# A two-layer fp32 decoder trunk on one core: statistics after the first lead product, and four plain chunks in the first feed-forward layer

## The chip, the core and the metric

The kernel runs on one core of a Trainium2 chip. The core has five engines, each with an instruction queue that it works off in order: TensorE (PE, matrix products into the PSUM banks), VectorE (DVE), ScalarE (ACT), GpSimd (POOL) and SyncE (SP, which here only starts transfers). They wait for one another through semaphores, and DMA queues bring data from memory to SBUF. The metric is the device time of one execution in microseconds (us); the time of a kernel is the median over its runs.

## The reference

All of it is float32, for 512 positions of 1024 channels:

```python
def reference(x, attn_norm, w_qkv, w_attn_out, pool_norm, w_pool_in, w_pool_group, pool_scale,
              ffn_norm, w_ffn_gate_up, w_ffn_down, final_norm):
    for i in range(DEPTH):                       # DEPTH = 2
        j = i // N_MIXERS                        # N_MIXERS = 2
        if i % N_MIXERS == 0:
            x = x + dilated_attention_mixer(rmsnorm(x, attn_norm[j]), w_qkv[j], w_attn_out[j])
        else:
            x = x + pooling_mixer(rmsnorm(x, pool_norm[j]), w_pool_in[j], w_pool_group[j], pool_scale[j])
        x = x + swiglu_ffn(rmsnorm(x, ffn_norm[i]), w_ffn_gate_up[i], w_ffn_down[i])
    return rmsnorm(x, final_norm)

def rmsnorm(x, g):
    y = x * lax.rsqrt(jnp.mean(x * x, axis=-1, keepdims=True) + RMS_EPS)
    return y * g

def swiglu_ffn(h, w_gate_up, w_down):            # 1024 -> 2 x 2816 -> 1024
    gu = h @ w_gate_up
    return (jax.nn.silu(gu[..., :D_FF]) * gu[..., D_FF:]) @ w_down
```

The attention mixer projects to queries, keys and values of three groups of 8 heads, attends in bands of three dilations and merges the groups. The pooling mixer projects 1024 to 1024, takes trailing means over 2, 4, 8 and 16 positions less the token for four groups of 256 channels, and maps each group by a 256 x 256 matrix.

## The kernel before

**Layout.** The activations stand transposed: eight blocks X[k] of 128 channels (partitions) by 512 positions. A normed input is never formed as such ahead of a product. The products take x times the norm's gain, and since the reciprocal root mean square is one number per position, that is per column, the results are multiplied by a row vector, named row, when they are taken out of PSUM. So a product can start before its statistics are known; only its result has to wait for row.

**Precision.** Every operand of PE is split into a high part (named hi, or whi for weights) and the rest (lo, wlo), both in a reduced format, and each product is three matmuls: whi x hi, whi x lo, wlo x hi (L272, L273, L275 in a plain product, L391 to L393 in a Strassen one). ACT makes the high part (L96), DVE the low one (L97).

**Two ways to multiply.** A plain product (Product, L253) of 8 blocks is 24 matmuls of 512 columns. A chunk of the feed-forward's up side, 128 hidden channels, needs a gate and an up product, so 48 matmuls. In the Strassen form (chain, L453) the same chunk is seven multiplications of 12 matmuls with 256 columns. Its weights come as sums of blocks of the matrix (Pair, L140): three loads by SP and one by POOL that adds into a buffer already loaded (L158), and DVE additions (L173, L174). Its inputs are sums and differences of the fully normed blocks: prepare(k), k = 0 to 3, makes them for blocks k and k + 4. It writes normed blocks hp and their sums tp (L501 to L508), and splits them into the operands tb, tt (two) and tn. They need row, and DVE and ACT work on them while PE does plain chunks. NPLAIN says how many of the 22 chunks are plain, before the Strassen ones. The multiplications of a chain run in the PSUM banks sum, ps and seed, and are taken out by ACT and DVE (half, gt, up).

**Weights** go through rings of buffers: 5 split blocks w, 2 halves, 4 raw blocks, 2 raw halves. pump() lets the next load and the next split start when a buffer is free, and is called after each product and each multiplication.

**Statistics.** While a block of x is completed, note (L322) makes its hi and lo operands (named h, in L318 and L319; for layer 3 n) and adds its square into acc (L310). rstd (L329) then sums acc over the partitions with four matmuls against ones (L335). DVE adds the epsilon (var, L340) and POOL raises to the power -0.5 (rcol, L342), which gives 512 numbers as [128 x 4]. spread (L345) brings them with four matmuls into a [128 x 512] tile in PSUM, and ACT copies that to row (L356).

**The entries.** A layer begins with begin (L359), which starts products over those blocks that are ready, and finish (L362): it completes them, takes the statistics, starts a third product with three blocks, does the spread, and completes the third. There are three such entries: to the feed-forward of layer 0 (L1151), to the pooling mixer (L1179) and to the feed-forward of layer 1 (L1239). In the text the pooling entry is the second.

```python
    def finish(lead, layer, ks):
        for f in lead:
            f.add(ks)
        r = rstd([acc[layer]])
        lead += begin(1, layer, range(3))
        row = row_of(spread(r))
        lead[-1].add(range(3, KC))
        return row
```

**What sets the order.** The code issues instructions in program order, and a scheduler of the framework (tile) places those of each engine, by its own model of when operands are ready, into the five queues; tc.issue_after pins the instructions issued in it behind a named one. On the chip each queue then runs strictly in that order. So a part that is issued elsewhere also moves its neighbours on the other engines.

Of the kernel before, what the change touches and what calls it, by code (L numbers as in the profile page):

```python
# [18 lines left out]
KC = D // P  # L19
# [17 lines left out]
K2 = KC // 2  # L37
NPLAIN = 5
WARM = 6
# [12 lines left out]
def trunk(ctx: ExitStack, tc: tile.TileContext, xT, norms, w_first, w_qk, w_qkp, w_v0, w_v0p, w_v12, w_out, w_pair, w_down, w_down0, w_down1, w_down2, w_pin, w_pgrp,  # L52
          consts, ident_in, invcnt_in, outT):
    nc = tc.nc
# [171 lines left out]
    def ffn_plan(layer):  # L226
        blocks = (w_down0, w_down1, w_down2)
        for g, (first, stop) in enumerate(GROUPS):
            for j in range(first + (g > 0), stop + 1 if g < 2 else FC):
                if j < NPLAIN:  # L230
                    plain_gu(layer, j)
                else:
                    pairs(w_pair[layer, j])
            if g < 2:
                for i in range(K2):
                    pairs(blocks[g][layer, i])
        for kind, i in TURNS:
            if kind == "block":
                pairs(blocks[2][layer, i])
            else:  # L240
                plain(w_down[layer, i])
# [11 lines left out]
    class Product:  # L253
# [7 lines left out]
        def add(self, ks, cols=slice(0, S), pos=None):  # L261
            for k in ks:
                if self.w:
                    w, c = self.w, k if pos is None else pos + k
                else:
                    self.held, c = self.held or weights(), k
                    w = self.held.t
# [6 lines left out]
                self.done += 1  # L274
                nc.tensor.matmul(self.p[:, cols], w[1][:, s], mh[:, cols], start=False, stop=self.done == self.n)  # L275
            if not self.w:
# [85 lines left out]
# [6 lines that stand above are left out]
        row = row_of(spread(r))  # L368
        lead[-1].add(range(3, KC))
        return row  # L370

    def both(t):
# [557 lines left out]
    with tc.tile_pool(name="fpool", bufs=1) as fpool:  # L930
# [16 lines left out]
        def ffn(layer, nxt, lead, row, wk):  # L947
# [85 lines left out]
            def plain_pair(j):  # L1033
# [3 lines left out]
                pu = gu()  # L1037
                if j == NPLAIN - 1:
                    for k in range(KC):
                        give((op, k))  # L1040
# [83 lines left out]
            for g, (first, stop) in enumerate(GROUPS):  # L1124
                for j in range(first + (g > 0), stop + 1 if g < 2 else FC):
                    if j < NPLAIN:
                        plain_pair(j)
                        if j < K2:
                            prepare(j)
                    else:  # L1130
                        strassen_pair(j)
# [18 lines left out]

        lead = begin(2, 1, range(KC - 1))  # L1151
        row = finish(lead, 1, [KC - 1])
        with tc.tile_pool(name="work0", bufs=1) as wk:
# [19 lines left out]
        with tc.tile_pool(name="pooling", bufs=6) as wk:  # L1173
# [4 lines left out]

            lead = begin(2, 2, range(KC - 1))  # L1179
            row = finish(lead, 2, [KC - 1])  # L1180
            Y = {}

# [197 lines left out]
```

## Time and profile before

| | |
|---|---|
| three timed runs | 1251.72, 1253.34, 1253.52 us; median 1253.34 |
| profiled execution | 1251.78 us; span 1250.0 us, mean granted PE clock 0.996 |
| PE | 1237.6 us busy, 99%, 9072 matmuls |
| DVE | 1013.6 us busy, 81% |
| ACT | 679.7 us busy, 54% |
| POOL | 154.9 us busy, 12% |
| transfers | 189.91 MB, mean 152 GB/s |

How to read the rows below. An instruction's row holds its start in us from the start of the span, its duration in us (of the first, with its time until the last ends, where several are put together with x), the engine, the line of the kernel, the operation, out<-in by the program's names, shapes, and in brackets how long the engine had been idle before and what released it. In the list of waits on PE the three numbers are the idle time in us in all, the number of waits, and the longest. In the table of stretches each engine has its busy time in us and the number of its instructions; the last two numbers are the DMA engines' mean share and the GB/s. SPq and POOLq are the engines' transfer queues. Since matmuls overlap one another, their own durations are longer than the distance at which they follow each other; a rate is taken from starts.

### The profile page before, as it was taken

Reading aid. Unit: us, or ns where it says so; the run is one execution under the profiler, and the core shown is the slowest. Engines: PE = TensorE matmul, PEld = TensorE weight load, DVE = VectorE, ACT = ScalarE, POOL = GpSimd, SP = SyncE. Lnnn points to the kernel's source line nnn. Section 1 sums busy time; section 2 is a strip of 40 time slices with the busy share of each in tenths; the row PEclk is TensorE's granted clock in tenths of the full one; section 3 lists DMA queues with packets and bytes.
Section 4 is the critical chain, followed back from the end, with each engine's and each line's share of the span. In section 5 each row is a group of like instructions: output and inputs, shape, how many; then the busy total and the mean of one; then the engine's idle time right before and its main releaser. Section 6 shows DMA issues by size and latency. Waiting matters only on the chain. (4 is left out here: it accounts for less than half of the span.)

```text
span 1250.0 us, 23243 instructions
## 1 busy us (share of the span) xinstructions
PE 1237.6 (99%) x9072; PEld 1174.0 (94%) x9072; DVE 1013.6 (81%) x1687; ACT 679.7 (54%) x1171; POOL 154.9 (12%) x147
## 2 busy tenths in 40 slices
PE   9999999999999999999999999999999999999997
PEld 7889999999999988889999999988789999999997
DVE  7987788878778846798777878798989877888876
ACT  6444554445455544466466557563446646656652
POOL 2011111112111010101111111000310111111100
PEclk9999999999999999999999999999999999999998
DMA  8336566655756434437776786653144777677742
GB/s 291 110 85 170 134 156 145 163 131 159 182 132 161 132 138 136 113 81 194 187 186 158 177 208 163 153 181 118 51 119 117 182 182 178 153 205 190 174 116 68
DMA packets 76719, 189.91 MB, mean 152 GB/s; under 512 B 7600, under 2 KB 15936, under 8 KB 76608
## 3 DMA queue, kind: packets, MB, share of 16 engines
q1 hardware_dynamic: 51696, 142.26, 35.7%
q0 software_dynamic: 24336, 45.63, 22.5%
q8 instruction: 71, 1.16, 0.4%
q10 hardware_dynamic: 576, 0.52, 0.1%
q14 instruction: 40, 0.33, 0.1%
HBM read 186.29 MB, written 2.10 MB: 151 GB/s over the span
## 5 line engine op out<-in xcount | busy, mean ns | idle before, releaser
L96 ACT ACTIVATE whi<-raw 128x1024 fp32r<-128x1024 f32 (+2 forms) x315 | 318.7, 1016 | 248.3 <-PE seed L392 76.1
L97 DVE TENSOR_TENSOR wlo<-raw,whi 128x1024 fp32r<-128x1024 f32 (+2 forms) x315 | 367.1, 1169 | 105.3 <-ACT whi L96 104.5
L158 POOL DMA_DIRECT2D raw<-w_pair x34 | 41.1, 1209 | 310.5 <-ACT whi L96 75.4
L391 PE MATMUL sum<-tt,whi 128*128 128x256 f32 x272 | 77.0, 283 | 1.5 <-ACT seed L477 0.8
L392 PE MATMUL sum<-tt,whi 128*128 128x256 f32 x272 | 76.7, 282 | 0.0
L393 PE MATMUL sum<-tt,wlo 128*128 128x256 f32 x272 | 76.5, 281 | 0.0
L96 ACT ACTIVATE halfhi<-rawhalf 128x512 fp32r<-128x512 f32 (+1 forms) x87 | 53.2, 612 | 19.8 <-PE sum L392 12.4
L173 DVE TENSOR_TENSOR raw<-raw 128x512 f32<-128x512 f32 (+1 forms) x87 | 57.6, 662 | 2.1 <-issue 2.0
L174 DVE TENSOR_TENSOR raw<-raw 128x512 f32<-128x512 f32 (+1 forms) x87 | 57.7, 663 | 0.2
L97 DVE TENSOR_TENSOR halflo<-rawhalf,halfhi 128x512 fp32r<-128x512 f32 (+1 forms) x87 | 57.6, 664 | 0.0
L158 POOL DMA_DIRECT2D raw<-w_down x24 | 28.9, 1206 | 215.2 <-DMA raw<-w_down 34.4
L391 PEld LDWEIGHTS sum<-tt,whi 128*128 128x128 f32 x272 | 51.4, 189 | 1.9 <-ACT seed L477 1.0
L477 ACT COPY seed<-sum 128x256 f32<-128x256 f32 x58 | 20.8, 359 | 57.7 <-PE sum L393 57.5
L392 PEld LDWEIGHTS sum<-tt,whi 128*128 128x128 f32 x272 | 51.3, 189 | 0.0
L393 PEld LDWEIGHTS sum<-tt,wlo 128*128 128x128 f32 x272 | 51.2, 188 | 0.0
L391 PE MATMUL sum<-hz,whi 128*128 128x256 f32 x160 | 45.4, 284 | 0.5 <-ACT seed L477 0.3
L392 PE MATMUL sum<-hz,whi 128*128 128x256 f32 x160 | 45.3, 283 | 0.0
L392 PE MATMUL seed<-hy,whi 128*128 128x256 f32 x160 | 45.3, 283 | 0.0
L393 PE MATMUL seed<-hy,wlo 128*128 128x256 f32 x160 | 45.2, 283 | 0.0
L393 PE MATMUL sum<-hz,wlo 128*128 128x256 f32 x160 | 45.2, 283 | 0.0
L391 PE MATMUL seed<-hy,whi 128*128 128x256 f32 x160 | 45.1, 282 | 0.0
L158 POOL DMA_DIRECT2D raw<-w_qkp x18 | 22.0, 1222 | 166.4 <-DMA raw<-w_qkp 102.1
(610 smaller groups left out, 4631.7 us busy)
## 6 DMA issues: line engine op xcount, KB each, us to landing
raw<-w_pair SPq DMA_DIRECT2D x78, 512.0 KB, 4.7
raw<-w_qkp SPq DMA_DIRECT2D x36, 512.0 KB, 4.6
raw<-w_pair POOLq DMA_DIRECT2D x34, 512.0 KB, 7.6
raw<-w_down SPq DMA_DIRECT2D x32, 384.0 KB, 3.9
raw<-w_v SPq DMA_DIRECT2D x18, 512.0 KB, 4.1
raw<-w_qkp POOLq DMA_DIRECT2D x18, 512.0 KB, 7.4
rawhalf<-w_pair SPq DMA_DIRECT2D x34, 256.0 KB, 4.5
raw<-w_down SPq DMA_DIRECT2D x16, 512.0 KB, 4.9
```

The lines of the kernel that those rows point to most:

```text
L96: nc.scalar.activation(hi, v, AF.Copy)
L97: nc.vector.tensor_tensor(lo, v, hi.bitcast(F32), op=OP.subtract)
L158: nc.gpsimd.dma_start(b.rearrange("p (a c) -> p a c", a=2), self.src[:, None, 3 * q:].to_broadcast([P, 2, q]), accum_op=OP.add)
L173: nc.vector.tensor_add(a[:, :q], a[:, :q], b[:, :q])
L174: nc.vector.tensor_add(a[:, q:2 * q], a[:, q:2 * q], a[:, :q])
L391: nc.tensor.matmul(dst, w.t[0][:, c], th, start=k == 0 and not onto, stop=False, skip_group_check=onto)
L392: nc.tensor.matmul(dst, w.t[0][:, c], tl, start=False, stop=False, skip_group_check=onto)
L393: nc.tensor.matmul(dst, w.t[1][:, c], th, start=False, stop=k == n - 1, skip_group_check=onto)
L477: nc.scalar.copy(e, c)
```

## The change

Three things change. The number of plain chunks becomes a number for each layer, NPLAIN = (4, 5): in layer 0 chunk 4 goes from plain to Strassen. With that the operands are made in another pattern in layer 0: prepare(0) after chunk 0, prepare(1) and prepare(2) after chunk 1, prepare(3) after chunk 2 and none after chunk 3, where it was one after each of chunks 0 to 3. Layer 1 keeps its five chunks and its pattern. And a new function enter takes the place of begin and finish at the first two entries: one product is run through all 8 blocks, the statistics follow it, a second product is begun with n blocks (5 in layer 0, all 8 at the pooling entry), the spread is pinned behind that product's last matmul so far, and then the product is completed. The third product is no longer started ahead of the chunks. Under the old code two products were run through seven blocks, then both completed, and then came the statistics. The third entry keeps finish.

```diff
--- before.py
+++ after.py
@@ -35,7 +35,7 @@
 NF = 4
 H2 = S // 2
 K2 = KC // 2
-NPLAIN = 5
+NPLAIN = (4, 5)
 WARM = 6
 NSOLO = 3
 BUFS = {"w": 5, "half": 2, "raw": 4, "rawhalf": 2}
@@ -227,7 +227,7 @@
         blocks = (w_down0, w_down1, w_down2)
         for g, (first, stop) in enumerate(GROUPS):
             for j in range(first + (g > 0), stop + 1 if g < 2 else FC):
-                if j < NPLAIN:
+                if j < NPLAIN[layer]:
                     plain_gu(layer, j)
                 else:
                     pairs(w_pair[layer, j])
@@ -272,7 +272,8 @@
                 nc.tensor.matmul(self.p[:, cols], w[0][:, s], mh[:, cols], start=self.done == 0, stop=False)
                 nc.tensor.matmul(self.p[:, cols], w[0][:, s], ml[:, cols], start=False, stop=False)
                 self.done += 1
-                nc.tensor.matmul(self.p[:, cols], w[1][:, s], mh[:, cols], start=False, stop=self.done == self.n)
+                self.tail = nc.tensor.matmul(self.p[:, cols], w[1][:, s], mh[:, cols], start=False,
+                                             stop=self.done == self.n)
             if not self.w:
                 pump(2)
             return self
@@ -368,6 +369,16 @@
         row = row_of(spread(r))
         lead[-1].add(range(3, KC))
         return row
+
+    def enter(layer, n):
+
+        lead = [Product(KC, stream(layer)).add(range(KC))]
+        r = rstd([acc[layer]])
+        lead += begin(1, layer, range(n))
+        with tc.issue_after(lead[-1].tail.ins):
+            row = row_of(spread(r))
+        lead[-1].add(range(n, KC))
+        return lead, row
 
     def both(t):
 
@@ -1035,7 +1046,7 @@
                 gt = wk.tile([P, S], F32, name="gt", bufs=1)
                 nc.vector.tensor_mul(gt, pg, row)
                 pu = gu()
-                if j == NPLAIN - 1:
+                if j == NPLAIN[layer] - 1:
                     for k in range(KC):
                         give((op, k))
                 up = wk.tile([P, S], F32, name="up", bufs=1)
@@ -1123,10 +1134,10 @@
 
             for g, (first, stop) in enumerate(GROUPS):
                 for j in range(first + (g > 0), stop + 1 if g < 2 else FC):
-                    if j < NPLAIN:
+                    if j < NPLAIN[layer]:
                         plain_pair(j)
-                        if j < K2:
-                            prepare(j)
+                        for k in ((0,), (1, 2), (3,), ())[j] if layer == 0 else range(j, min(j + 1, K2)):
+                            prepare(k)
                     else:
                         strassen_pair(j)
                 if g < 2:
@@ -1148,8 +1159,7 @@
                 drop("a")
             return over, act
 
-        lead = begin(2, 1, range(KC - 1))
-        row = finish(lead, 1, [KC - 1])
+        lead, row = enter(1, 5)
         with tc.tile_pool(name="work0", bufs=1) as wk:
             scratches.append(lambda name: wk.tile([P, S], F32, tag="hid", name=name, bufs=2))
             ffn(0, 2, lead, row, wk)
@@ -1176,8 +1186,7 @@
             def ftile(name, n=S):
                 return wk.tile([P, PAD + S], F32, tag="f", name=name)[:, :n]
 
-            lead = begin(2, 2, range(KC - 1))
-            row = finish(lead, 2, [KC - 1])
+            lead, row = enter(2, KC)
             Y = {}
 
             def pool(g):
```

How this moves instructions is read from the order in the queues. **POOL, at the entry of layer 0**: x are loads of the residual stream, raw<-w_pair accumulating loads of weights, rcol the power of the statistics. Before:

```order
L888 DMA x_4906<-xT 128x512
L888 DMA x_4907<-xT 128x512
L1163 DMA invcnt_9799<-invcnt_in 128x16
L342 TENSOR_TENSOR rcol_5668<-var_5666,nhalf_78 128x4
L158 DMA raw_5707<-w_pair 128x2x512
L158 DMA raw_5825<-w_pair 128x2x512
L158 DMA raw_6000<-w_pair 128x2x512
```

and now:

```order
L899 DMA x_4906<-xT 128x512
L899 DMA x_4907<-xT 128x512
L1173 DMA invcnt_9855<-invcnt_in 128x16
L158 DMA raw_5628<-w_pair 128x2x512
L343 TENSOR_TENSOR rcol_5641<-var_5639,nhalf_78 128x4
L158 DMA raw_5738<-w_pair 128x2x512
L158 DMA raw_5931<-w_pair 128x2x512
```

rcol stood directly behind the early loads. Now the accumulating load of chunk 4's weights, raw_5628, stands ahead of it.

**PE, at the pooling entry.** Here seed and ps are the products in the banks of these names, h the input blocks, ps<-ones,acc the sum over squares. Before:

```order
L272 MATMUL ps_9820<-h_9790,whi_9676 128x512
L273 MATMUL ps_9820<-h_9790,whi_9676 128x512
L275 MATMUL ps_9820<-h_9790,wlo_9677 128x512
L272 MATMUL seed_9842<-h_9790,whi_9692 128x512
L273 MATMUL seed_9842<-h_9790,whi_9692 128x512
L275 MATMUL seed_9842<-h_9790,wlo_9693 128x512
L335 MATMUL ps_9878<-ones_77,acc_9475 128x1 x4
L272 MATMUL ps_9887<-h_9472,whi_9708 128x512
```

and now:

```order
L272 MATMUL seed_9914<-h_9681,whi_9748 128x512
L273 MATMUL seed_9914<-h_9681,whi_9748 128x512
L273 MATMUL ps_9876<-h_9846,whi_9732 128x512
L275 MATMUL ps_9876<-h_9846,wlo_9733 128x512
L275 MATMUL seed_9914<-h_9681,wlo_9749 128x512
L336 MATMUL ps_9905<-ones_77,acc_9531 128x1 x4
L272 MATMUL seed_9914<-h_9789,whi_9748 128x512
L273 MATMUL seed_9914<-h_9789,whi_9748 128x512
L275 MATMUL seed_9914<-h_9789,wlo_9749 128x512
L272 MATMUL seed_9914<-h_9810,whi_9748 128x512
```

The last block (h_9790 before, h_9846 now) was multiplied for both products ahead of the sum over squares. Now the sum comes directly behind the first product's part with it, with the second product's blocks partly drawn ahead and the rest after.

**DVE, at the end of the operands of layer 0**, up to the first Strassen chunk. tt and tn are operands of the last prepare, gt, up and hr of a plain chunk, t, hx, hy, hz and hu operands for the down side, up<-sum,half the removal of a chain's result. Before:

```order
L97 TENSOR_TENSOR tt_5966<-tp_5957,tt_5966 128x512
L97 TENSOR_TENSOR tn_5883<-hp_5956,tn_5883 128x256
L97 TENSOR_TENSOR tt_5969<-tp_5957,tt_5969 128x512
L97 TENSOR_TENSOR hx_6111<-hr_5721,hx_6111 128x256
L1000 TENSOR_TENSOR t_6112<-hr_5721 128x256
L97 TENSOR_TENSOR hy_6135<-hr_5721,hy_6135 128x512
L1036 TENSOR_TENSOR gt_6010<-ps_5974,row_5685 128x512
L97 TENSOR_TENSOR wlo_6007<-raw_5824,whi_6006 128x1024
```

and now:

```order
L97 TENSOR_TENSOR tt_5897<-tp_5888,tt_5897 128x512
L97 TENSOR_TENSOR tt_5900<-tp_5888,tt_5900 128x512
L1047 TENSOR_TENSOR gt_5941<-ps_5905,row_5664 128x512
L173 TENSOR_TENSOR raw_5737<-raw_5737,raw_5738 128x512
L1053 SCALAR_TENSOR_TENSOR up_5972<-seed_5943,row_5664 128x512
L174 TENSOR_TENSOR raw_5737<-raw_5737 128x512
L97 TENSOR_TENSOR wlo_5969<-raw_5738,whi_5968 128x1024
```

and further down, at the first chain:

```order
L97 TENSOR_TENSOR hy_6126<-hr_5885,hy_6126 128x512
L97 TENSOR_TENSOR hz_6070<-t_6042,hz_6070 128x512
L97 TENSOR_TENSOR hu_6099<-t_6042,hu_6099 128x256
L1094 TENSOR_TENSOR up_5977<-sum_5979,half_5978 128x256
L97 TENSOR_TENSOR wlo_6038<-raw_5737,whi_6037 128x1024
L1088 TENSOR_TENSOR gt_5976<-seed_5982,half_5978 128x256
```

Behind the last operand (tt_5969 before, tt_5900 now) stood the work of chunk 4 as a plain one (gt_6010) and the down side's operands. Now chunk 3's gt_5941 and up_5972 stand there, and a dozen rows later the first chain's up.

## The prediction

> **What bounds the kernel now.** I read four views in this order: the page's engine table, who waited for whom on TensorE (PE), the timelines of the places that the diff touches, and busy time by stretch.
>
> ```profile
> PE 1237.6 (99%) x9072; PEld 1174.0 (94%) x9072; DVE 1013.6 (81%) x1687; ACT 679.7 (54%) x1171; POOL 154.9 (12%) x147
> ```
>
> ```profile
> PE sum L391 <- ACT seed L477: 1.1, 2, 0.8
> PE ps L350 <- POOL rcol L342: 1.1, 1, 1.1
> PE sum L391 <- ACT seed L469: 0.8, 2, 0.7
> PE ps L272 <- ACT h L318: 0.3, 1, 0.3
> PE ps L273 <- DVE n L319: 0.2, 1, 0.2
> ```
>
> The first row says that PE is the bound, the second fence (us in total, times, longest) that it hardly waits: 3.5 us in these rows, of which only the last two and a fraction of the second lie where the diff works. So this change can win in two ways alone: less matmul time, and the few tenths that PE loses around the two entries. It can lose wherever another engine, now with less room, makes PE wait.
>
> **The change part by part.** First the matmul time. Starts on PE, each the first matmul of its piece:
>
> ```profile
> 545.17 0.39 PE L272 MATMUL seed<-h,whi 128*128 128x512 f32 x1
> ...
> 550.61 0.28 PE L391 MATMUL sum<-tb,whi 128*128 128x256 f32 x1
> ...
> 570.81 0.28 PE L391 MATMUL sum<-tb,whi 128*128 128x256 f32 x1
> ...
> 580.81 0.28 PE L391 MATMUL sum<-tb,whi 128*128 128x256 f32 x1
> ```
>
> One whole product (24 matmuls of 512 columns) runs from 545.17 to 550.61: 5.44 us, 0.227 us a matmul. A plain chunk is two, 10.88 us. The third Strassen chunk (84 matmuls of 256 columns) runs from 570.81 to 580.81: 10.00 us, 0.119 us a matmul; the first two together took 20.20, so the start of the row of chunks costs 0.20 extra already. Chunk 4 of layer 0 turns from plain to Strassen: 10.00 - 10.88 = **-0.88 us**. In columns it is 84 x 256 against 48 x 512, an eighth less; the trace gives back a third of that, since a column costs more in the short matmuls.
>
> The Trainium skill (TensorE: Matmul & The Clock Gate, "Wait — 56ns, not 53.3ns?") puts a warm matmul at its columns over 2.4 GHz plus about 2.5 ns. By it, an estimate, this term would be 84 x 109.2 - 48 x 215.8 ns = -1.19 us. The rows above show a larger fixed part per matmul, and the measurement decides: -0.88 stays.
>
> **Second, the entry of layer 0** (enter(1, 5)), where the row of statistics comes from. Quoted: PE; then DVE (VectorE); POOL; the SP and POOL rows of loads; and one POOL row and two DVE rows of the other entry.
>
> ```profile
> 493.93 0.39 PE L272 MATMUL ps<-h,whi 128*128 128x512 f32 x1
> ...
> 504.81 0.94 PE L335 MATMUL ps<-ones,acc 128*128 128x1 f32 x8
> 505.62 0.49 PE L272 MATMUL ps<-h,whi 128*128 128x512 f32 x1
> ...
> 508.09 1.16 PE L350 MATMUL ps<-ident,rcol 128*128 128x128 f32 x8
> 509.00 0.47 PE L272 MATMUL ps<-h,whi 128*128 128x512 f32 x1
> ```
>
> ```profile
> 496.80 0.69 DVE L310 TENSOR_TENSOR acc<-acc,sq 128x512 f32<-128x512 f32 x1
> 505.79 0.16 DVE L340 TENSOR_SCALAR var<-ps 128x4 f32<-128x4 f32 x1 [8.31 <-PE ps L335]
> 505.90 2.36 DVE L97 TENSOR_TENSOR wlo<-raw,whi 128x1024 fp32r<-128x1024 f32 x2
> 509.91 0.69 DVE L1036 TENSOR_TENSOR gt<-ps,row 128x512 f32<-128x512 f32 x1 [1.65 <-ACT row L356]
> ```
>
> ```profile
> 506.04 1.99 POOL L342 TENSOR_TENSOR rcol<-var,nhalf 128x4 f32<-128x4 f32 x1 [7.38 <-DVE var L340]
> 513.55 1.28 POOL L158 DMA_DIRECT2D raw<-w_pair  x1 [5.52 <-DVE hp L501]
> 524.96 1.22 POOL L158 DMA_DIRECT2D raw<-w_pair  x1 [10.13 <-DVE tp L508]
> ```
>
> ```profile
> 496.25 0.33 SPq L132 DMA_DIRECT2D raw<-w_pair  x1
> ...
> 508.29 0.33 SPq L155 DMA_DIRECT2D raw<-w_pair  x1
> ...
> 520.70 0.33 SPq L155 DMA_DIRECT2D raw<-w_pair  x1
> ```
>
> ```profile
> 849.43 1.03 POOL L342 TENSOR_TENSOR rcol<-var,nhalf 128x4 f32<-128x4 f32 x1 [42.51 <-DVE var L340]
> ```
>
> ```profile
> 849.60 2.36 DVE L97 TENSOR_TENSOR wlo<-raw,whi 128x1024 fp32r<-128x1024 f32 x2 [0.27 <-ACT whi L96]
> 852.89 0.69 DVE L1191 TENSOR_TENSOR u<-ps,row 128x512 f32<-128x512 f32 x1 [0.93 <-ACT row L356]
> ```
>
> Now one whole product, 493.93 + 5.44 = 499.37, stands ahead of the sum over squares. Its input acc was done at 497.49 (496.80 + 0.69), so this has 1.9 us to spare. The sum takes 0.81 (504.81 to 505.62): 500.18. var follows the sum's start by 0.98: 500.35, done 500.51. Fifteen matmuls later, at 503.59, PE reaches the spread.
>
> rcol now stands behind a chunk-4 load on POOL, which the old order put after it. That accumulating load waits for the first load into the same buffer, issued by SP at 496.25 (the same slot in the ring, the same 512 KB). From such an issue to POOL's start the rows give 4.26 us (520.70 to 524.96): 500.5. I add 0.3 for the spread of such gaps: 500.8. POOL then needs 1.22 to 1.28: about 502.05, which is 1.5 us after var. rcol itself took 1.99 us beside a DVE subtraction that reads two buffers (505.90), and 1.03 where it began ahead of one (849.43). Between 502 and 505 DVE has nothing left in its order but to wait for row, so I take 1.03: rcol at 503.1, half a microsecond before PE asks. PE's idle before the spread (505.62 plus nine matmuls of about 0.24 is 507.8, the spread began at 508.09) goes: **-0.3 us**. If the load needs 5.26 us (508.29 to 513.55 was such a gap) and rcol 1.99, rcol is done at 504.8 and PE idles 1.2: +0.9.
>
> The Trainium skill (SBUF — State Buffer, "Who interferes with whom") speaks against this order: it says that a DVE instruction with two SBUF inputs and a GpSimd instruction that reads SBUF exclude each other for the whole instruction. The weight split that frees the next buffer would then hold the accumulating load until about 501.9, rcol would end near 504.2, and this term, an estimate by that page, would be +0.3. The 1.99 against 1.03 agrees with the rule; the 1.22 and 1.28 of loads issued while DVE was full do not show it for loads. So I keep -0.3 and 0.9 as the far end.
>
> Then the spread takes 0.91 (508.09 to 509.00) and row reaches DVE 1.82 after the spread's start: 505.4 instead of 509.91, **4.5 us earlier**.
>
> **Third, what covers the operands.** The Strassen operands of layer 0 are now due one chunk earlier. Work of DVE by stretch (columns: PE, PE loads, DVE, ACT, POOL busy, clock, DMA):
>
> ```profile
> 509.90:544.50 34.60, 34.60 (x155) 28.61 (x154) 34.42 (x57) 18.90 (x29) 3.70 (x3) 1.00 0.47 118
> 853.00:886.00 33.00, 33.00 (x144) 26.82 (x143) 32.59 (x69) 12.80 (x18) 1.47 (x1) 1.00 0.43 133
> 886.00:906.00 20.00, 19.66 (x82) 14.70 (x81) 18.72 (x34) 10.21 (x16) 8.55 (x6) 1.00 0.09 29
> ```
>
> DVE ran without a pause from row's arrival to the last operand at 544.5, 57 instructions in 34.6 us, and the first chain began at 550.61, 6.1 us later. In the new order the same stretch holds 54: the fourth chunk's gt, up and product fall behind it, 3 x 0.61 us. So 505.4 + 32.8 = 538.2. PE arrives at 503.59 + 0.91 + nine matmuls (2.04) + six products (32.64) = 539.2. The cover shrinks from 6.1 us to 1.0, and it holds, since the last operand is not read before the chain's fifth multiplication. What is late next is the evictions: 16 DVE instructions, about 8.4 us, stand between the last operand and the subtraction that empties the sum bank, due 6 x 1.43 = 8.6 us after the chain's start: DVE is there at about 547.6 and done at 548.0, PE asks at 547.8. I take **+0.3** over the 0.2 that the old start cost, with -0.2 (no wait at all) and +1.4 (0.5 us in each of three chains) as ends.
>
> **Fourth, the pooling entry** (enter(2, KC)).
>
> ```profile
> 844.01 0.39 PE L272 MATMUL seed<-h,whi 128*128 128x512 f32 x1
> ...
> 851.17 1.05 PE L350 MATMUL ps<-ident,rcol 128*128 128x128 f32 x8
> ```
>
> ```profile
> 843.90 0.75 DVE L319 SCALAR_TENSOR_TENSOR h<-x,nrm,h 128x512 fp32r<-128x512 f32 x1
> 844.56 0.69 DVE L310 TENSOR_TENSOR acc<-acc,sq 128x512 f32<-128x512 f32 x1
> ```
>
> The wait for the seventh block (L272 <- ACT h, 0.3 above) stays. The eighth block is now asked for at 844.01, and its low half at 844.70; it was done at 844.65. The sum over squares comes at 845.4, acc was done at 845.25. So nothing is lost, by 0.05 and 0.15 us; +0.4 is the far end. The spread follows the sum (0.81) and twelve matmuls at 849.0 instead of 851.17, and rcol has 2.7 us for its 1.0 to 2.0. Row reaches DVE at 850.7 instead of 852.89. In the pooling stage DVE is 99% busy up to 886 and then late: PE did 144 matmuls in 33.00 us, 0.229 each, in the one stretch; the 82 of the next would take 18.8 us at that rate and took 20.00, so about 1.2 us were lost. DVE's 2.2 us of lead should remove most: **-0.6** (0 to -1.0).
>
> **Sum:** -0.88 - 0.3 + 0.3 - 0.6 = -1.5 us. The profiled execution took 1251.78 us (span 1250.0), which becomes 1250.3. It is at the lower end of the three timed runs (1251.72 to 1253.52, median 1253.34); against their median the forecast is **1251.8 us**.
>
> **The rivals.** (1) *DVE becomes the bound at the first chains*: for it speaks the cover of 1.0 us; against it that operands are read one after another. Then +1.4 stands for +0.3 and the pooling relief is none: -0.88 - 0.3 + 1.4 = +0.2, 1253.5 us. (2) *POOL's order decides, and the kernel is slower*: rcol waits for a load. For it speaks that POOL's order has turned; against it the gap of 4.26 us. Without the entry's term the sum is -1.2; PE's idle at the spread was 0.3, so the kernel loses from an idle of 1.5 us on, rcol done after 505.1, which is a load needing over 6 us to POOL's start. I price it at 7 us, near the 6.7 that the load issued at 514.95 took to land (last fence), and rcol at 1.99: 496.25 + 7.0 + 1.28 + 1.99 = 506.5, 2.9 us of idle: +1.4, 1254.7 us. (3) *All small waits go*: -0.88 - 0.3 - 0.2 - 1.0 = -2.4, 1250.9 us. (4) *The statistics do not come earlier*: DVE gets row at 509.91 as now, and its operands last until 509.9 + 32.8 = 542.7, 3.5 us after PE's 539.2. Against it: sum, var and spread all stand a product further ahead. -0.88 + 3.5 - 0.6 = +2.0, 1255.3 us. It is the far end of (2).
>
> ```profile
> raw<-w_pair SPq DMA_DIRECT2D x1, 512.0 KB, 6.7
> ```
>
> **Chances.** Forecast 0.58, (1) 0.20, (2) with (4) 0.09, (3) 0.13. Ends of all terms are -2.4 and +1.8 or so; laid on the lowest and highest of the runs they give 1249.3 and 1255.3, and since they hardly come together I say 1249.5 to 1254.9. About 0.2% (2.5 us, below 1250.8 or above 1255.8) is what a measurement of this kernel can tell from no change; no case reaches it by its own sum alone, (3) comes near it. Faster 0.20 (most of (3), and an eighth of the forecast, whose median may fall a microsecond low as one of the three runs did), same 0.74, slower 0.06 (half of (2), if its price is larger than worked out).
>
> **What would show it.** In the new profile: 84 matmuls of 256 columns more and 48 of 512 fewer, the first chain near 539; the spread near 503.6 with no wait for rcol, whose POOL row begins after a load at about 502; DVE's first gt near 505.4; the sum bank's wait (up, L1094 of the changed kernel) under 0.5 us; the pooling spread near 2 us ahead of the sum's old distance, and no PE wait for n (L320 there). I am wrong if the chain waits for tb, tt or tn, if rcol ends later than 505, or if the gap between matmuls shows the bound elsewhere.

## The result

| kernel | median | runs | ratio to before, 95% interval |
|---|---|---|---|
| before | 1251.99 us | 14, 1250.91 to 1254.33 | |
| the change | 1254.83 us | 14, 1253.87 to 1255.63 | 1.0018, 1.0011 to 1.0025 |
| the change, second series | 1253.41 us | 11, 1250.38 to 1256.91 | 1.0002, 0.9991 to 1.0012 |

The prediction was 1251.8 us and no change or slightly faster, worked out as 1.5 us less than before. The first series is slower by 0.18% (2.3 us; the medians lie 2.8 us apart), clear of its interval and on the wrong side; the second cannot be told from no change. The first median, 1254.83 us, still lies just inside the range that was given, 1249.5 to 1254.9. So two questions stand: what the change costs, and what moves a kernel by 1.4 us from series to series.

The engine table of the changed kernel, and what PE waited for (total us, times, longest):

```profile
PE 1236.9 (99%) x9108; PEld 1175.1 (94%) x9108; DVE 1016.7 (81%) x1691; ACT 682.8 (55%) x1178; POOL 154.2 (12%) x148
```

```profile
PE ps L273 <- DVE n L320: 2.1, 3, 0.9
PE sum L402 <- ACT seed L488: 1.9, 3, 0.8
PE sum L402 <- ACT seed L480: 1.4, 2, 1.3
```

PE is busy 0.7 us less, and there are 36 matmuls more, as 84 for 48 must give. But the waits for n have risen from 0.2 to 2.1 us, and those for ACT's copies in the chains from 1.9 to 3.3.

Where the time went is read from the same matmul in both traces. Six places of the kernel before, on PE: a multiplication ahead of the second group's down chains in layer 0, one behind them, the first product over h for the pooling mixer, the first chain of layer 1, a multiplication behind the second group's down chains there, and the last sum of squares.

```profile
690.99 0.28 PE L393 MATMUL sum<-tt,halflo 128*128 128x256 f32 x1
...
743.89 0.28 PE L393 MATMUL sum<-tt,halflo 128*128 128x256 f32 x1
...
836.29 0.39 PE L272 MATMUL ps<-h,whi 128*128 128x512 f32 x1
...
953.15 0.28 PE L391 MATMUL sum<-tb,whi 128*128 128x256 f32 x1
...
1144.15 0.28 PE L392 MATMUL sum<-tt,halfhi 128*128 128x256 f32 x1
...
1238.16 0.24 PE L335 MATMUL ps<-ones,total 128*128 128x1 f32 x1
```

The same in the changed kernel, with the start of its first lead product ahead (493.93 before):

```profile
494.49 0.39 PE L272 MATMUL ps<-h,whi 128*128 128x512 f32 x1
...
690.41 0.28 PE L404 MATMUL sum<-tt,halflo 128*128 128x256 f32 x1
...
744.23 0.28 PE L404 MATMUL sum<-tt,halflo 128*128 128x256 f32 x1
...
836.65 0.39 PE L272 MATMUL ps<-h,whi 128*128 128x512 f32 x1
...
954.81 0.28 PE L402 MATMUL sum<-tb,whi 128*128 128x256 f32 x1
...
1147.22 0.28 PE L403 MATMUL sum<-tt,halfhi 128*128 128x256 f32 x1
...
1241.25 0.24 PE L336 MATMUL ps<-ones,total 128*128 128x1 f32 x1
```

The differences of the starts, and their steps:

| stretch | changed minus before, at its end | step |
|---|---|---|
| up to the first lead product | +0.56 | +0.56 |
| entry and first chunks of layer 0 | -0.58 | **-1.14** |
| behind the second down group, layer 0 | +0.34 | **+0.92** |
| up to the pooling entry | +0.36 | 0.0 |
| pooling mixer and entry of layer 1 | +1.66 | **+1.30** |
| layer 1, to behind its second down group | +3.07 | **+1.41** |
| up to the last sum of squares | +3.09 | 0.0 |

The span is only 2.2 us longer, since the end is 0.9 us shorter: the last spread took 2.08 us in the one execution and 1.16 in the other.

```profile
1240.87 2.08 PE L350 MATMUL ps<-ident,rcol 128*128 128x128 f32 x8 [1.10 <-POOL rcol L342]
```

```profile
1243.96 1.16 PE L351 MATMUL ps<-ident,rcol 128*128 128x128 f32 x8 [1.10 <-POOL rcol L343]
```

The kernel before, profiled once more, has 1.80 us there, so this end varies without any change. It goes with the granted PE clock: during that spread it was 0.50 in the first profile of before and 1.00 in the change's. The +0.56 of the start is there after the first 10 us, among matmuls that the change doesn't touch.

**Layer 0 did as forecast.** PE, POOL and DVE of the changed kernel at the entry:

```profile
499.94 0.95 PE L336 MATMUL ps<-ones,acc 128*128 128x1 f32 x8
...
504.29 1.05 PE L351 MATMUL ps<-ident,rcol 128*128 128x128 f32 x8
...
539.89 0.28 PE L402 MATMUL sum<-tb,whi 128*128 128x256 f32 x1
```

```profile
501.31 1.22 POOL L158 DMA_DIRECT2D raw<-w_pair  x1 [2.08 <-DMA raw<-w_pair]
502.08 1.53 POOL L343 TENSOR_TENSOR rcol<-var,nhalf 128x4 f32<-128x4 f32 x1
```

```profile
501.03 1.23 DVE L97 TENSOR_TENSOR wlo<-raw,whi 128x1024 fp32r<-128x1024 f32 x1
506.01 0.69 DVE L1047 TENSOR_TENSOR gt<-ps,row 128x512 f32<-128x512 f32 x1 [3.75 <-ACT row L357]
```

With the 0.56 of the start taken off, the load begins on POOL at 500.75, the spread on PE at 503.73, row reaches DVE at 505.45, and the first chain starts at 539.33. rcol is done at 503.61, before PE asks at 504.29, and PE waits for nothing.

**The pooling stage did not.** DVE before, in the stretch in which the last products over y are taken out (x) and the low halves n of the next operands are made, and POOL beside it:

```profile
887.22 1.23 DVE L97 TENSOR_TENSOR wlo<-raw,whi 128x1024 fp32r<-128x1024 f32 x1 [0.32 <-ACT whi L96]
...
888.43 0.74 DVE L1216 SCALAR_TENSOR_TENSOR x<-ps,nrm,x 128x512 f32<-128x512 f32 x1
889.15 0.75 DVE L1216 SCALAR_TENSOR_TENSOR x<-seed,nrm,x 128x512 f32<-128x512 f32 x1
889.82 0.68 DVE L97 TENSOR_TENSOR y<-u,y 128x512 fp32r<-128x512 f32 x1
890.41 2.45 DVE L319 SCALAR_TENSOR_TENSOR n<-x,nrm,n 128x512 fp32r<-128x512 f32 x2
```

```profile
890.60 3.41 POOL L310 TENSOR_TENSOR acc<-acc,sq 128x512 f32<-128x512 f32 x2 [10.04 <-ACT sq L309]
```

The same in the changed kernel: the split by ACT that DVE waits for, then DVE, POOL and PE:

```profile
886.54 1.06 ACT L96 ACTIVATE whi<-raw 128x1024 fp32r<-128x1024 f32 x1 [1.41 <-PE seed L273]
```

```profile
887.63 1.23 DVE L97 TENSOR_TENSOR wlo<-raw,whi 128x1024 fp32r<-128x1024 f32 x1 [1.04 <-ACT whi L96]
888.78 0.68 DVE L97 TENSOR_TENSOR y<-u,y 128x512 fp32r<-128x512 f32 x1
889.38 0.75 DVE L1225 SCALAR_TENSOR_TENSOR x<-ps,nrm,x 128x512 f32<-128x512 f32 x1
890.04 0.74 DVE L1225 SCALAR_TENSOR_TENSOR x<-seed,nrm,x 128x512 f32<-128x512 f32 x1
890.97 0.75 DVE L1225 SCALAR_TENSOR_TENSOR x<-ps,nrm,x 128x512 f32<-128x512 f32 x1 [0.18 <-PE ps L275]
891.63 3.44 DVE L320 SCALAR_TENSOR_TENSOR n<-x,nrm,n 128x512 fp32r<-128x512 f32 x2
```

```profile
891.55 4.67 POOL L311 TENSOR_TENSOR acc<-acc,sq 128x512 f32<-128x512 f32 x3 [11.34 <-ACT sq L310]
```

```profile
892.16 0.40 PE L272 MATMUL ps<-n,whi 128*128 128x512 f32 x1
893.44 0.50 PE L273 MATMUL ps<-n,whi 128*128 128x512 f32 x1 [0.88 <-DVE n L320]
...
894.01 0.40 PE L272 MATMUL ps<-n,whi 128*128 128x512 f32 x1
895.13 0.51 PE L273 MATMUL ps<-n,whi 128*128 128x512 f32 x1 [0.73 <-DVE n L320]
```

Three things are to be seen. DVE's lead is gone before this place: it stands 1.04 us (0.32 before) for ACT's half of a weight split, and ACT stands 1.41 us for PE ahead of it. Then the scheduler, given the earlier row, has put a third x, for which DVE waits for PE, ahead of the first n. And so both n now fall beside POOL's addition: the two take 3.44 us where they took 2.45, as only the second was slowed. PE, which comes to n at 892.16, stands 1.05 and 0.90 us (start to start, less the usual 0.23).

**Behind the down chains** the order on all engines is the same in both kernels. ACT before and after, in layer 1, at the split of the same weights:

```profile
1133.00 1.06 ACT L96 ACTIVATE whi<-raw 128x1024 fp32r<-128x1024 f32 x1 [0.36 <-PE seed L392]
```

```profile
1136.55 1.06 ACT L96 ACTIVATE whi<-raw 128x1024 fp32r<-128x1024 f32 x1 [2.25 <-DMA raw<-w_pair]
```

In the changed kernel's execution the load came too late; ACT stood, and behind it stood the copy (seed) for which PE waits. Here is how dense the loads are, by the table of stretches of the kernel before (the last two columns, DMA share and GB/s):

```profile
660.00:690.00 30.00, 30.00 (x255) 30.00 (x254) 25.07 (x43) 20.12 (x39) 3.64 (x3) 1.00 0.70 156
700.00:740.00 40.00, 38.53 (x316) 37.71 (x316) 31.40 (x55) 20.47 (x35) 4.82 (x4) 1.00 0.81 208
```

While PE runs the short down chains of the second group (9 matmuls a multiplication rather than 12, 7.7 us a chain), the loads of the next, longer chunks (10 us a chain) are already being asked for.

### The profile page after: what moved, and what is told of

It reads as the page before. It is cut to its first block, busy times and chain, and to the rows that moved or that the text cites. A ratio compares the mean times of both kernels' runs of the same rounds, so it can differ in the third digit from the quotient of the medians.

```text
span 1252.2 us, 23337 instructions
## 1 busy us (share of the span) xinstructions
PE 1236.9 (99%) x9108; PEld 1175.1 (94%) x9108; DVE 1016.7 (81%) x1691; ACT 682.8 (55%) x1178; POOL 154.2 (12%) x148
## 3 DMA queue, kind: packets, MB, share of 16 engines
q8 instruction: 71, 1.16, 0.4%
## 5 line engine op out<-in xcount | busy, mean ns | idle before, releaser
L402 PE MATMUL sum<-tt,whi 128*128 128x256 f32 x280 | 79.4, 284 | 2.9 <-ACT seed L488 1.6
L403 PE MATMUL sum<-tt,whi 128*128 128x256 f32 x280 | 78.8, 281 | 0.0
L402 PEld LDWEIGHTS sum<-tt,whi 128*128 128x128 f32 x280 | 52.8, 189 | 3.9 <-ACT seed L488 2.0
L403 PEld LDWEIGHTS sum<-tt,whi 128*128 128x128 f32 x280 | 52.8, 188 | 0.0
```

The lines of the kernel that those rows point to most:

```text
L402: nc.tensor.matmul(dst, w.t[0][:, c], th, start=k == 0 and not onto, stop=False, skip_group_check=onto)
L403: nc.tensor.matmul(dst, w.t[0][:, c], tl, start=False, stop=False, skip_group_check=onto)
```

## The experiments

**First: is the loss fixed, and in which part?** The change unaltered, its two parts apart, and the chunks without the new entry. Only the layer 0 part:

```diff
-            lead, row = enter(2, KC)
+            lead = begin(2, 2, range(KC - 1))
+            row = finish(lead, 2, [KC - 1])
```

Only the pooling part keeps enter(2, KC), with NPLAIN = (5, 5), the old pattern of operands and the old entry of layer 0. The fourth keeps NPLAIN = (4, 5) and the new pattern, with both old entries.

> The changed kernel once more, for a second profile. Theory A (the losses at the two places behind down chains, about 0.9 us near 724 to 744 and 1.4 us near 1137 to 1143 of the changed kernel, come with how the loads happen to land, and vary from execution to execution): the profile shows other amounts there, at least one of the two by 0.5 us or more away. Theory B (they are fixed by the change): 0.7 to 1.2 and 1.2 to 1.7 us again. In both the pooling stage loses 1.2 to 1.6 us against the kernel before, since that comes with the order. Time 1254.5, 0.18% above before.

> Only the layer 0 part of the change (four plain chunks, new pattern of operands, statistics after the first lead product), the pooling entry as before. Theory A (the pooling stage's new order is the systematic loss): PE is 1.1 us ahead from the first chains on, as in the changed kernel, the pooling stage loses nothing, and the time is 1250.9 us, 0.999 of before. Theory B (the layer 0 part costs later, through loads behind the down chains): 1252.5 to 1253.5, at or above before.

> Only the pooling entry of the change, layer 0 as before. Theory A: the pooling stage loses 1.2 to 1.6 us on PE, in waits for n, and the time is 1253.4 us, 1.001 of before. Theory B (pooling is not what costs): 1251.4 to 1252.2.

> Only four plain chunks and the new pattern of operands in layer 0, both entries as before. Row then comes to DVE at about 510.5 and its operands last until 543, while PE is at the first chain at 540: by the prediction's own steps the first chain waits 2 to 3.5 us for operands, and the time is 1251.99 - 0.9 + 2 to 3.5 = 1253.1 to 1254.6. Rival: the chains read their operands one after another, the wait is under 1 us, and the time is 1251.1 to 1252.

Before in this series: 1252.56 us.

| kernel | median | ratio, interval | PE's waits in the down group's wake, both layers |
|---|---|---|---|
| the change again | 1253.41 | 1.0002, 0.9991 to 1.0012 | 2.5 |
| layer 0 part only | 1252.31 | 0.9996, 0.9987 to 1.0005 | 3.8 |
| pooling part only | 1254.34 | 1.0015, 1.0007 to 1.0024 | 2.9 |
| chunks only | 1253.63 | 1.0006, 0.9997 to 1.0015 | 3.7 |

The last column is the sum in us of two rows of each kernel's list of waits, those of the chains' sum bank for ACT's copies (1.9 in the first profile of before, 3.3 in the change's; 0.5 of each lies elsewhere, at the end of layer 0). Single waits are given below from start to start, which is 0.1 to 0.3 us more than the list has. In the change's second profile they are:

```profile
PE sum L402 <- ACT seed L480: 1.4, 2, 1.2
PE sum L402 <- ACT seed L488: 1.1, 2, 0.8
```

The waits for n were 1.05, 0.90 and 0.61 us in this profile, as in the change's first, and the same again in the pooling part alone; in the two kernels with the old pooling entry they were 0.27 and 0.35 or so, as before. The step of the stretch with the pooling mixer was +1.30, +1.33 and +1.30 us in these three profiles. So the waits for n are fixed and belong to the order. The waits behind the down chains are not fixed: in layer 1 the change had 1.05 us in its first profile and 0.22 in its second, as theory A had it for at least one of the two places; in layer 0 they moved less (2.6 and 2.3).

The pooling part alone came out where theory A had put it or somewhat higher. The layer 0 part alone is where neither theory had put it: its trace gains 1.07 us between the first lead product and 690 us, and then loses 3.1 us in a single wait behind the down chains, so that nothing of it is left in this profile and half of it by the ratio.

The chunks-only kernel decides a step of the prediction's rival (4). Row reached DVE at 510.75 and the last operand (tt) was made at 543.8, but the first chain started at 540.56 and went on without any wait for operands. The wait of 2 to 3.5 us is refuted: the chain reads its operands one after another, and here the cover was 3 us short without cost. The time, 1253.63 us, lies all the same where the wait of 2 to 3.5 us had put it; that is no support for the wait, since the trace has 3.2 us of waits behind the down chains instead.

**Second: the order in the pooling stage, and the loads.** The pin: the third x is put behind both n in DVE's order.

```diff
+                    with tc.issue_after(made[2].ins) if g == 1 else nullcontext():
-                    nc.vector.scalar_tensor_tensor(X[m], f.p, nrm[:, 5, m:m + 1], X[m],
-                                                   op0=OP.mult, op1=OP.add)
+                        nc.vector.scalar_tensor_tensor(X[m], f.p, nrm[:, 5, m:m + 1], X[m],
+                                                       op0=OP.mult, op1=OP.add)
...
-                    scaled(3, m, t[:, 0], t[:, 1])
+                    made[g] = scaled(3, m, t[:, 0], t[:, 1])
```

(scaled returns the instruction that makes n.) The cut, in before and in the change, leaves out the accumulating loads of chunks 15 to 18 of both layers, so that the sums of weight blocks of these chunks lack a term:

```diff
             pairs(w_pair[layer, j])
+            units[-1][0].light = j in (15, 16, 17, 18)
...
+            if self.light:
+                return
             nc.gpsimd.dma_start(b.rearrange("p (a c) -> p a c", a=2),
```

> The change, with one addition in the pooling stage: the removal of the next product (x) is pinned on DVE behind the low parts n of both blocks before it. Theory A (the pooling loss is the order in which DVE makes n and removes products): the first two waits for n, 1.05 and 0.90 us in every profile of the new entry, fall under 0.3 us each, the stage loses under 0.6 us against before, PE is ahead of before by 0.3 to 1.0 us at the first chain of layer 1, and the time falls 1 us below the change's. Theory B (the waits come from the time at which row arrives or from ACT's weight split, not from that order): they stay at 0.8 to 1.1 us each.

> The kernel before without the accumulating loads of chunks 15 to 18 of both layers, so their sums of weight blocks lack one term: eight of 512 KB. Theory A (the waits behind the second group of down chains come from loads that land late where the DMA engines are 0.83 to 0.91 busy): those waits, 1.8 us in the first profile of before, go to under 0.4 us, and the time falls by 0.7 to 2 us. Theory B (they come from ACT's and DVE's own queues): they stay above 1 us.

> The changed kernel with the same eight accumulating loads left out. With the waits behind the down chains gone from both, what is left between this and the same cut of the kernel before is the layer 0 part (-1.1 us) and the pooling stage (+1.3): +0.2 us, between -0.3 and +0.7. If the layer 0 part itself makes the loads land later (the rival), the cut helps the change by 1 us or more beyond what it helps before.

> The kernel before once more, for a second profile of the waits behind the down chains. If they are chance, they differ from the first profile's (1.8 us in layer 0, none in layer 1) by 0.5 us or more in at least one layer; if they belong to the kernel, they are the same within 0.2 us. The pooling stage's waits for n are 0.3 us at most in both.

Before in this series: 1252.76 us (35 runs).

| kernel | median | runs | ratio, interval |
|---|---|---|---|
| change, pinned | 1252.40 | 1248.21 to 1254.01 | 0.9996, 0.9988 to 1.0005 |
| before, cut | 1250.36 | 1249.93 to 1251.59 | 0.9984, 0.9975 to 0.9993 |
| change, cut | 1250.43 | 1249.62 to 1251.21 | 0.9983, 0.9974 to 0.9991 |
| before again | 1252.83 | 1251.14 to 1253.55 | 0.9998, 0.9988 to 1.0008 |

The same stretch of the cut kernel before, by the table of stretches:

```profile
700.00:740.00 40.00, 40.00 (x333) 39.58 (x332) 32.82 (x56) 23.05 (x37) 1.20 (x1) 1.00 0.48 163
```

With the DMA engines at 0.48 instead of 0.81, PE does 333 matmuls in the 40 us and not 316, the sum of the two rows of waits falls to the 0.5 us that lie elsewhere, the time falls by 0.16% (2.0 us), and the runs lie closer together, with a standard deviation of 0.52 us (11 runs) against 0.82 (35 runs of before). Theory A holds for the wait: it comes from loads that land late. A high DMA share alone does not make it, though: the profile of the pinned change, with every load in its old place, has 0.78 and 206 GB/s in this stretch and no such wait. In the uncut kernel before, profiled again, they were 2.0 us in all as in the first, but lay otherwise: 0.56 us in layer 1, where the first had none.

```profile
PE sum L391 <- ACT seed L477: 1.5, 3, 0.8
...
PE sum L391 <- ACT seed L469: 0.5, 2, 0.4
```

And with the cut, before and change are alike in their medians: +0.07 us, where -1.1 and +1.3 had given +0.2. Their two profiles are not alike, and show what the list of waits leaves out. In the cut change's profile the stretch with the waits for n costs 2.9 us and not 1.3. Here it is, by the table of stretches; the third number from the end is the granted PE clock:

```profile
888.60:892.00 3.40, 1.79 (x7) 0.88 (x6) 3.40 (x4) 1.66 (x4) 3.24 (x3) 1.00 0.02 5
892.05:895.40 3.35, 3.35 (x9) 2.67 (x8) 3.35 (x11) 0.63 (x1) 0.76 (x1) 0.50 0.00 0
```

The first row holds the two waits. In the second the granted clock is 0.50, and matmuls of 512 columns start 0.43 us apart instead of 0.23. That is 1.6 us on top of the waits. The profile of the pooling part with the cut, below, has the same (clock 0.50 from 893.8 to 897.2, stretch +2.9 us), and the chunks-only kernel had 3.4 us at 0.50 in layer 0, at 727.4, right behind its wait of 2.2 us. The other profiles with the same waits for n kept the full clock there. So the waits for n are fixed, but what they cost is not: the stretch is 1.3 to 1.4 us longer in four profiles, 2.9 in two. That the standing of PE brings the clock down is likely from these places, but no run separates it.

The pin does to the waits what theory A says. DVE of the pinned kernel:

```profile
887.66 0.75 DVE L320 SCALAR_TENSOR_TENSOR n<-x,nrm,n 128x512 fp32r<-128x512 f32 x1
...
888.95 1.19 DVE L320 SCALAR_TENSOR_TENSOR n<-x,nrm,n 128x512 fp32r<-128x512 f32 x1
890.08 1.75 DVE L1209 TENSOR_TENSOR s<-u 128x512 f32<-128x512 f32 x1
```

The first n takes 0.75 us again and the second 1.19, and it is an addition s, for which PE doesn't wait, that is slowed to 1.75 beside POOL. The waits of 1.05 and 0.90 are gone, and the stretch costs 0.22 us more than before, where it was 1.30. But DVE's wait of 1.03 us for the weight split ahead of it is still there: the lead is lost with and without the pin. The time of the whole pinned kernel, 1252.40 us, can't be told from before; its profile was its fastest run, 4.2 us below its median.

The Trainium skill (SBUF — State Buffer, "Who interferes with whom") says that a DVE instruction with two SBUF inputs and a GpSimd instruction that reads SBUF hold each other up. The 0.75 us of n alone against 1.7 beside POOL, and the 1.75 of s, agree with it. The same page limits the rule to GpSimd instructions that read, and reports that a DVE tensor_tensor, as the subtraction of a weight split is, did not stall a DMA. The prediction had priced the rule for the accumulating load all the same; the load of 1.22 us at 501.31, beside the subtraction at 501.03, shows no such blocking.

**Third: the parts in the quiet kernel, and a version with less density.** Layer 0 only, pooling only and the pinned change with the cut; and the pinned change, whole, with one chunk moved:

```diff
                     for i in range(K2):
+                        if g == 1 and i == 2:
+                            strassen_pair(15)
                         down(g, i)
```

(with the same move in the plan of the loads, and chunk 15 taken from its old place).

> Only the layer 0 part of the change, and the accumulating loads of chunks 15 to 18 left out as in the two cut kernels before. Theory A (layer 0 gains 1.1 us, pooling loses 1.3): 1250.36 - 1.1 = 1249.2 us, 0.9975 of the whole kernel before. Rival (layer 0 gains nothing that reaches the end): 1250.2 to 1250.6.

> Only the pooling entry of the change, with the same eight loads left out. Theory A: 1250.36 + 1.3 = 1251.7 us. Rival (the pooling order costs nothing in the end): 1250.2 to 1250.6.

> The whole change with the pin in the pooling stage, with the same eight loads left out. Theory A: the layer 0 part's -1.1 us and about -0.3 from the pooling stage: 1248.9 us. Rival: the pin only moves the wait, 1250.0 to 1250.5.

> The change with the pin, whole, and chunk 15 of both layers moved from behind the four short down chains of the second group to between the second and the third of them, so that the large loads of chunks 15 to 18 are asked for over 41 us rather than 31. If the waits behind the down chains come from the loads' density there, they fall from 1.8 to 3.1 us in layer 0 to under 1 us, and the time to 1250 us, 0.998 of before. If they do not hang on it, the time stays at 1252.4 us.

Before in this series: 1252.22 us (25 runs).

| kernel | median | runs | ratio, interval |
|---|---|---|---|
| layer 0 only, cut | 1249.29 | 1248.50 to 1250.13 | 0.9978, 0.9968 to 0.9987 |
| pooling only, cut | 1251.51 | 1250.76 to 1252.66 | 0.9990, 0.9981 to 0.9999 |
| pinned, cut | 1249.15 | 1248.46 to 1249.89 | 0.9975, 0.9966 to 0.9984 |
| pinned, chunk moved, whole | **1248.47** | 1248.16 to 1248.81 | **0.9969, 0.9958 to 0.9980** |

The three cut kernels came out within 0.3 us of what theory A gave. Against the cut kernel before (1250.36) the layer 0 part is worth -1.07 us and the pooling part +1.15; together +0.08, and the cut change showed +0.07. These are medians of two series, whose kernel before stood at 1252.76 and 1252.22. By the ratios, which rest on the uncut kernel before of each series, it is -0.06% and +0.06%, the same sign with 0.75 us each; the intervals of the two overlap that of 0.9984. So the times give the signs and the size only roughly; the traces say -1.1 in every kernel with the layer 0 part, and +1.3 or, with the fall of the clock, +2.9. In the same way the pin takes 1.28 us from the cut change by the medians and 1.0 by the ratios, again with overlapping intervals, and leaves the layer 0 gain.

The moved chunk gave more than was expected, 1248.47 against 1250, with its 6 runs within 0.7 us. It is the fastest kernel of this study. Its stretches:

```profile
700.00:740.00 40.00, 40.00 (x337) 39.84 (x336) 33.20 (x58) 22.11 (x37) 4.82 (x4) 1.00 0.78 196
1105.00:1145.00 40.00, 40.00 (x336) 39.85 (x335) 33.39 (x56) 23.56 (x41) 6.02 (x5) 1.00 0.75 197
```

Nearly the same loads as before, 196 GB/s, but PE does not stand in either stretch; a wait of 0.7 us at 744 is left of 1.8 to 3.1.

**Fourth: before and change, whole and quiet.** What the cut showed was tried without leaving anything out: the same move of chunk 15 in the kernel before and in the change as it is.

> The kernel before, whole, with chunk 15 of both layers between the second and the third short down chain, and nothing else. If the waits behind the down chains are what scatters its time, the runs lie within 1.5 us of one another and their median at 1249.9 us (the pinned and interleaved change's 1248.47, and 1.4 more for layer 0 and the pooling stage). Rival (the interleaving alone does little): 1251.5 to 1252.5.

> The change, whole and without the pin, with chunk 15 moved in the same way. Theory A (in a quiet kernel the change is -1.1 us in layer 0 and +1.2 in the pooling stage): within 0.4 us of the kernel before with the same move. Rival (the first series' +2.3 us is the change's own, in layer 0 too): 1.5 us or more above it.

Before in this series: 1253.01 us (21 runs). With the move, the kernel before took 1250.80 us (1249.87 to 1252.51; ratio 0.9985, 0.9976 to 0.9994), between the 1249.9 that was expected and the rival's 1251.5; its profile has none of the waits behind the down chains. The change took 1249.92 (1248.85 to 1252.05; 0.9977, 0.9968 to 0.9986). The change is 0.9 us below before, outside the 0.4 that theory A gave and on the other side from the rival's 1.5 above; the intervals overlap. The runs lie within 2.6 and 3.2 us, not within 1.5, so some scatter is left. The waits for n were 1.04, 0.90 and 0.62 us once more, and the stretch cost 1.36. That the two parts of the change cost 2.3 us by themselves is refuted; what they cost together with the old place of chunk 15 is not settled by this.

## Why the prediction was wrong

- **The matmul term** (-0.88), **the layer 0 entry** (-0.3) and **the first chains** (+0.3) came out: -1.14 us in the trace against -0.9. The load on POOL began at 500.75 and was forecast for 500.8, row reached DVE at 505.45 (505.4), the chain started at 539.33 (539.2), all less the start's 0.56. With the -0.88 as priced, the rest is -0.40 up to the first chain and +0.14 from there to 690 us.
- **The cover of the operands** needed no care: rival (1) starts from its shrinking, and rival (4), with its 3.5 us, charges a chain for operands that it reads later. The chunks-only run shows no wait with the last operand 3.3 us behind the chain's start.
- **Rival (2)** named the right turn of POOL's order and the wrong price: the load started on POOL 4.5 us after SP's issue at 496.81, not 7, and rcol was in time.
- **The failed step is the fourth, "the pooling entry: -0.6 (0 to -1.0)".** It measured +1.3 in the trace and +1.15 by the medians of the cut kernels (+0.75 by their ratios), and the sign of being right that it named, no PE wait for n, failed with 2.1 us. Row was copied 2 us earlier, as forecast (ACT at 850.59 less 0.36, against 852.27). But the step took DVE's 2.2 us for a lead that would last to the end of a 50 us stage. DVE took the first product out only 1.55 us earlier (851.70 less 0.36, against 852.89), behind a weight split for which it had stood 2.41 us, and at 886 it stands 1.04 us for another split, for which ACT has to wait for PE. There the rest of the lead ends. And it took the order in the rest of the stage for unchanged: the scheduler's order there had turned, which could have been read ahead, and a low half n that PE waits for had come to lie beside POOL's addition. The far ends that the step gave its two parts were 0 and +0.4, so no term held +1.3; that the first median fell inside the range is luck.
- **What no step looked at** is the wake of the second down group, 0.92 and 1.41 us in this pair of profiles. The list of waits of before named it in its first and third rows of ACT's copies (1.1 and 0.8 us), and the prediction set these aside as lying where the diff doesn't work. They are not the change's alone: they vary in the kernel before too, and with chunk 15 moved the change isn't slower. By the lists of waits of the uncut kernels with the old place of chunk 15 they range from nothing to 3.3 us, more than the sum that was forecast, and in this pair the two steps add up to 2.3 us, as much as the whole difference.
- **Left open:** whether the whole kernel with the layer 0 part meets those late loads more often than the kernel before. Four uncut profiles with four plain chunks and the old place of chunk 15 had 2.5 to 3.8 us in the two rows of waits, two profiles of before 1.9 and 2.0, the pooling part alone 2.9, and the pinned change, which has the layer 0 part too, only 0.5. That is too few to tell. Waits that vary by chance from run to run would hardly keep all 14 runs of the change's first series within 1.8 us of one another and 1.4 us above the second; what held them there is not known.

## What to carry to other kernels

A lead given to an engine lasts only to its next wait on the bound engine; before pricing it, follow that engine's queue to the first instruction that waits for a buffer which the bound engine frees. Where a scheduler sets the order, an earlier arrival changes the order behind it, so the rows after the moved step are read as closely as the step itself, above all for instructions that two engines slow for each other. And a wait that comes and goes with the landing of loads is a scatter of the measurement: take it away in both kernels before comparing a microsecond.

## What the runs showed that was not expected

Small waits can blur a measurement more than they lengthen the kernel: with the DMA share between 700 and 740 us at 0.48 instead of 0.81, the standard deviation of the runs fell from 0.82 to 0.52 us. The number of bytes matters less than when they are asked for: with 196 GB/s in place of 208, and one long chunk between the short ones, PE did 337 matmuls in 40 us, as many as with the loads left out (333). And a wait can cost more than its own length: twice, 1.9 us of waits for n (from start to start) were followed by 3.4 us at a granted clock of 0.50, which cost another 1.6 us. The change with pin and move gains 0.31% over before, more than the change was ever forecast to bring.
